# Decoder block with a 16,384-expert mixer on one core: other dense tiles, another pacing of the gathers, sums of the dense experts kept in PSUM

## The chip, the cores and the metric

One core of one Trainium2 chip runs the whole kernel in one launch. The metric is device time in microseconds, the median of several runs. A difference of about 1% is what a measurement of this kernel can tell from no change.

## What is computed

One decoder layer over 1,024 tokens of width 1,024, all in float32. Three token mixers (stick-breaking attention, dilated attention, attention to 256 memory tokens) share one normalised input, are gated by sigmoids, summed and projected. Then comes the expert mixer, which fills most of the time:

```python
q = (hf @ w_q).reshape(T, PEER_HEADS, 2, PEER_HALF)          # 8 heads, two halves of 128
sc = jnp.einsum('thpd,hpkd->thpk', q, subkeys)               # 128 sub-keys for each half
# top 16 of each half, top 16 of their 256 sums -> idx (T, 8, 16) of 16,384 experts, gate = softmax
act = jax.nn.gelu(jnp.einsum('chkd,cd->chk', u[ic], hc), approximate=False)
w = (gc * act)
out = jnp.einsum('chk,chkd->cd', w, v[ic])                   # u, v: (16384, 1024) float32
```

Each token takes 128 of the 16,384 experts: 128 rows of `u` and 128 rows of `v`, 4 KB each.

## The kernel before

The tokens are 8 tiles of 128. The **front** (everything up to the choice of experts) runs in three groups of tiles, `GROUPS = (2, 3, 3)`: tiles 0 and 1, 2 to 4, 5 to 7. Within a group the stages follow one another: norm, `stick_breaking`, `dilated` with `memory_attn`, `gating` (24 gate projections and 24 branch projections), `out_proj`, `ffn_norm`, `select` (query projection and scores). The top-k work of a group's later tiles runs as a side generator (`topk`, in `side`), a piece at each fill, after the group's `select`.

The expert mixer is done in two ways.

- **Six sparse tiles** go through `Experts`. One step takes one expert slot of 128 rows: GpSimd gathers 128 rows of `u` and 128 rows of `v` by indirect DMAs (line 1090, 512 KB each), VectorE multiplies and sums `u` with the token (line 1144), ScalarE applies Gelu, TensorE adds the weighted `v` rows up (line 1170). A tile has 128 steps, all six 768. A step's rows lie in rings of 5 and 6 buffers.
- **Two dense tiles**, `DENSE = (4, 6)`, are multiplied by all 16,384 experts in 128 blocks of 128 experts (`dense`). A block takes 24 matmuls of 256 columns (line 1188, the u product: each float32 operand is split in two parts, a high and a low one, and three partial products are taken), Gelu, a product with the gate matrix, and 12 matmuls of 512 columns (the v sums). The splits are a ScalarE copy and a VectorE subtraction (line 1269). Every two blocks the sums are added from PSUM to the tile `acc` (line 1317).

The gate matrix of a dense tile holds the weight of each expert for each token (`gate_matrix`): for every token two one-hot rows are made on VectorE (lines 1213 and 1215), multiplied on TensorE, copied by ScalarE into a tile `g` and written to DRAM as `gd`, in 4 blocks of 32 tokens; the dense loop loads `gd` back. The matrix of tile 4 is made inside the gating and `out_proj` stages of the third group (`rest`, which lets `want` count the dense tiles of earlier groups); that of tile 6 after the front, in `dense`, before the 128 blocks. Those fills have no other filler work: only gather steps run beside them.

All engines take their instructions in program order, and the order is written by a planner (the last loop of the kernel). It keeps two clocks, `pe` and `dma`: every fill adds its estimated TensorE time times `slow` to the one and its loaded bytes over `bw` to the other; every gather step adds `TOKEN_NS` and `TOKEN_BYTES / bw`.

```python
            while filler[0] is not None and (dma > pe or pe < due):
                a, b = fill(1)
                pe += a
                dma += b
            pe += TOKEN_NS
            dma += TOKEN_BYTES / bw[0]
            if ex.step():
```

So a stage of P ns of estimated TensorE time and M bytes of loads gets about (P x slow - M / bw) / (TOKEN_BYTES / bw - TOKEN_NS) gather steps. Steps that are left when the fillers have ended run alone. PSUM has 5 rotating banks (`bank`), 3 more belong to the gathers.

Of the kernel before, what the change touches and what calls it, by code (L numbers as in the profile page):

```python
# [7 lines left out]
F32 = mybir.dt.float32  # L8
# [3 lines left out]
AF = mybir.ActivationFunctionType  # L12
# [5 lines left out]
D = 1024  # L18
T = 1024
NT = T // 128  # L20
KD = D // 128
# [6 lines left out]
F32R = mybir.dt.float32r  # L28
MANUAL = dict(engines={mybir.EngineType.Activation})
GROUPS = (2, 3, 3)  # L30
DENSE = (4, 6)
ND = len(DENSE)
PAUSE = 4
LAG = 1


BW = 295.0, 360.0
SLOW = 1.38, 1.1
TOKEN_NS, TOKEN_BYTES = 700.0, 128 * 8192 + 3 * 8192.0
LEAST = 3000.0  # L40
SPLIT = (0,)
AHEAD = 2
# [34 lines left out]
def block_kernel(ctx: ExitStack, tc: tile.TileContext, io):  # L77
    nc = tc.nc
# [24 lines left out]
    TD = ND * 128  # L103
    cost = [0.0]
# [3 lines left out]
    def bank():  # L108
        return ps.tile([128, 512], F32, name="bank")
# [12 lines left out]
    def actf(out, in_, f, **kw):  # L122
        s = SETS.get(f)
        if s and table[0] != s:
            nc.scalar.preload_act_table_set(s)  # L125
            table[0] = s
        nc.scalar.activation(out, in_, f, **kw)  # L127
# [50 lines left out]
    gofs, gwid, gnum, o = [], [], [], 0  # L178
# [54 lines left out]
    xres = dram.tile([NT, 128, D], F32, name="xres")  # L233
# [3 lines left out]
    gd = dram.tile([TD // 32, 128, 128, 32], F32, name="gd")  # L237
# [7 lines left out]
    def load(out, src):  # L245
        count(out)
        nc.sync.dma_start(out, src)
# [762 lines left out]
    def phase1(gidx, n0, G, out):  # L1010
        N = G * 128
        pipe = Pipe()
        weights = Weights(gidx)
        hT = wide.tile([128, 8, NMAX], F32, name="wide")
        load(hT[:, :, :N], io["xT"][:, :, n0 * 128:n0 * 128 + N])
        norm = norm_T(hT, N, g_mix, hT)
        if gidx == 0:
            memT = big.tile([128, 8, MEM], F32, name="big")
            load(memT, io["memT"])
            mh = big.tile([128, 8, MEM], F32, name="big")  # L1020
            yield from norm_T(memT, MEM, g_mem, mh)
            kv = memory_kv(pipe, weights, both(gidx, mh, MEM))
            next(kv)
            next(norm)
            yield next(kv)
            next(norm)
            yield next(kv)
            yield next(kv)
            hT = both(gidx, hT, N)
            yield from kv  # L1030
            weights.ahead = AHEAD
            gap_tables()
        else:
            yield from norm
            hT = both(gidx, hT, N)
        oT = act.tile([128, 10, NMAX], F32, name="oT")
        yield from stick_breaking(pipe, weights, hT, n0, G, oT)
        mem = memory_attn(pipe, weights, hT, n0, G, oT)
        yield from dilated(pipe, weights, hT, n0, G, oT, mem)
        yield from mem  # L1040
        mT = wide.tile([128, 8, NMAX], F32, name="wide")
        pipe.flush()
        yield from gating(pipe, weights, hT, N, oT, mT)
        x2 = wide.tile([128, GMAX, D], F32, name="wide")
        yield from out_proj(weights, mT, n0, G, x2)
        h2T = [big.tile([128, 8, NS], F32, name="big") for _ in subs(G)]
        yield from ffn_norm(x2, n0, G, h2T)
        yield from select(pipe, weights, both(gidx, h2T, N), n0, G, out)
# [137 lines left out]
    def mmr(out, lhsT, rhs, **kw):  # L1186
        cost[0] += rhs.shape[-1] / 2.4 + 3
        nc.tensor.matmul(out, lhsT, rhs, **kw)  # L1188
# [51 lines left out]
    C = 2  # L1240

    def dense():
        st = ctx.enter_context(ExitStack())
        dp = st.enter_context(tc.tile_pool(name="dp", bufs=2))
        late_pool.append(dp)
        while len(stored) < ND:
            cost[0] += 1500
            yield
        hh = dp.tile([128, KD, TD], F32R, name="hh", bufs=1)
        hl = dp.tile([128, KD, TD], F32R, name="hl", bufs=1)  # L1250
        acc = dp.tile([128, ND, D], F32, name="acc", bufs=1)
        for i in range(ND):
            r = dp.tile([128, KD, 128], F32, name="ur")
            load(r, h2d[i])
            c = slice(i * 128, (i + 1) * 128)
            actf(hh[:, :, c], r, AF.Copy)
            nc.vector.tensor_sub(hl[:, :, c], r, hh[:, :, c])
            load(acc[:, i, :], xres[DENSE[i]])

        def raw(src, name):  # L1260
            r = dp.tile([128, C, D], F32, name=name)
            load(r, src)
            return r

        def split(r, x, name, bufs):
            hi = dp.tile([128, D], F32R, name=name + "h", bufs=bufs)
            lo = dp.tile([128, D], F32R, name=name + "l", bufs=bufs)
            actf(hi, r[:, x], AF.Copy)
            nc.vector.tensor_sub(lo, r[:, x], hi)  # L1269
            return hi, lo  # L1270

        us, vs, ws = {}, {}, {}
        ur = {0: raw(io["uT"][0], "ur")}
        us[0] = split(ur[0], 0, "u", 2)
        while next(gates) < ND:
            cost[0] += 800
            yield
        for c in range(128 // C):
            if c + 1 < 128 // C:
                ur[c + 1] = raw(io["uT"][c + 1], "ur")  # L1280
            vr = raw(io["vd"][c], "vr")
            for x in range(C):
                e = c * C + x
                if e % 8 == 0:
                    gt = dp.tile([128, TD // 32, 8, 32], F32, name="g")
                    load(gt, gd[:, :, e:e + 8, :].rearrange("b p i t -> p b i t"))
                if e + 1 < 128:
                    us[e + 1] = split(ur[(e + 1) // C], (e + 1) % C, "u", 2)
                vs[x] = split(vr, x, "v", C)
                uh, ul = us.pop(e)  # L1290
                a = bank()
                for k in range(KD):
                    kc = slice(k * 128, (k + 1) * 128)
                    mmr(a[:, :TD], uh[:, kc], hh[:, k, :], start=k == 0, stop=False)
                    mmr(a[:, :TD], ul[:, kc], hh[:, k, :], start=False, stop=False)
                    mmr(a[:, :TD], uh[:, kc], hl[:, k, :], start=False, stop=k == KD - 1)
                w = dp.tile([128, TD], F32, name="w")
                actf(w, a[:, :TD], AF.Gelu)
                nc.vector.tensor_mul(w.rearrange("p (b t) -> p b t", t=32),
                                     w.rearrange("p (b t) -> p b t", t=32), gt[:, :, e % 8, :])  # L1300
                wh = dp.tile([128, TD], F32R, name="wh", bufs=C)
                wl = dp.tile([128, TD], F32R, name="wl", bufs=C)
                actf(wh, w, AF.Copy)
                nc.vector.tensor_sub(wl, w, wh)  # L1304
                ws[x] = wh, wl
                yield
            for i in range(ND):
                for half in range(2):
                    o = bank()
                    f = slice(half * 512, (half + 1) * 512)  # L1310
                    for x in range(C):
                        wh, wl = (z[:, i * 128:(i + 1) * 128] for z in ws[x])
                        vh, vl = (z[:, f] for z in vs[x])
                        mmr(o, wh, vh, start=x == 0, stop=False)
                        mmr(o, wh, vl, start=False, stop=False)
                        mmr(o, wl, vh, start=False, stop=x == C - 1)
                    nc.vector.tensor_add(acc[:, i, f], acc[:, i, f], o)  # L1317
                    yield
        for i in range(ND):
            nc.sync.dma_start(io["out"][DENSE[i]], acc[:, i, :])  # L1320

    ready, side, stored, late_pool = [], [], [], []

    def sides(n):
        while n and side:
# [4 lines left out]
    gates = gate_matrix()  # L1330

    def rest():
        n0 = built = 0
        odd = False
        for g in range(len(GROUPS)):
            for stage in phase1(g, n0, GROUPS[g], ready):
                if stage and built < ND:

                    want = sum(n < n0 for n in DENSE)
                    while len(stored) < want:  # L1340
                        sides(1)
                    odd = not odd
                    for _ in range(999 if stage == 2 else 1 + odd):
                        if built < want:
                            built = next(gates)
                yield
            n0 += GROUPS[g]
        front.close()
        slow[0], bw[0] = SLOW[1], BW[1]
        yield from dense()  # L1350

    filler = [rest()]
    slow, bw = [SLOW[0]], [BW[0]]
    pe = dma = due = 0.0

    def fill(nside):
# [12 lines left out]
    while done < NT - ND or filler[0] is not None:  # L1369
        if ex.more():  # L1370

            due = max(due + LEAST, pe - LEAST)
            while filler[0] is not None and (dma > pe or pe < due):
                a, b = fill(1)
# [66 lines left out]
```

## Time and profile before

| | us |
|---|---|
| three runs | 3843.71, 3854.40 (median), 3871.12 |
| the profiled execution: its own time | 3814.17 |
| its span | 3812.4 |
| front of the first group, no gathers | 0 to 500 |
| fronts of the second and third group, with gathers | 500 to 2525 |
| gate matrix of tile 6 | 2525 to 2745 |
| the 128 dense blocks | 2745 to 3615 |
| gather steps alone | 3615 to 3812 |

The stages were placed by the first and last start of their VectorE lines. The profile gives for any stretch the busy time of each engine, the granted TensorE clock (PEclk, 1.00 is full speed), the mean busy share of the 16 DMA engines and what they moved in GB/s. Matmuls are pipelined, so that a busy TensorE need not be at its peak.

### The profile page before, as it was taken

The numbers are of one execution on the slowest core, as the hardware profiler recorded it, in microseconds if no ns is written. First come the engines' busy times: TensorE is split into PE (matmuls) and PEld (weight loads), VectorE is DVE, ScalarE is ACT, GpSimd is POOL, SyncE is SP. The second block draws the span as 40 slices with busy tenths as digits, with TensorE's granted clock in tenths as the row PEclk, the third lists the DMA queues.
The fourth block names the chain that finished last, engine by engine and source line by source line (L and its number), as shares of the span: only waits on it lengthen the run. The fifth ranks groups of instructions, "written<-read, shape, count | busy, mean of one in ns | idle before, by whom it ended". The sixth has DMA issues, their size and how long they took to land.

```text
span 3812.4 us, 61678 instructions
## 1 busy us (share of the span) xinstructions
PE 3276.5 (86%) x23106; PEld 2403.4 (63%) x23106; DVE 2542.9 (67%) x6405; ACT 1402.9 (37%) x2769; POOL 1712.1 (45%) x1544
## 2 busy tenths in 40 slices
PE   7999778988999798879898998864699999999944
PEld 6889755655556575656555556642478878888700
DVE  5443785555444478875555655699788888888844
ACT  4442435544211225555443222222344444444400
POOL 0000045646566465645454555553633434334476
PEclk9999888999999899989898999885799999999955
DMA  4345578889799997879897999877989999999899
GB/s 153 119 122 168 191 258 305 329 282 356 281 397 395 343 393 268 326 266 322 292 349 268 378 362 376 327 277 274 342 327 366 367 348 362 366 375 369 330 372 345
DMA packets 347010, 1186.38 MB, mean 311 GB/s; under 512 B 38808, under 2 KB 80792, under 8 KB 327256
## 3 DMA queue, kind: packets, MB, share of 16 engines
q0 software_dynamic: 221184, 805.40, 56.9%
q1 hardware_dynamic: 102960, 338.34, 24.8%
q10 hardware_dynamic: 22568, 38.70, 2.7%
q8 instruction: 182, 2.98, 0.3%
q14 instruction: 116, 0.95, 0.1%
HBM read 1142.58 MB, written 39.71 MB: 310 GB/s over the span
## 4 chain that ended last, share of the span: by engine, by line
PE 56%; DVE 16%; issue 10%; DMA 8%; ACT 4%; POOL 3%; another core or an unknown queue 2%; ACTq 1%; POOLq 0%; SPq 0%; DVEq 0%
PE bank L116 29%; PE bank L1188 17%; PE po L1170 6%; DVE u L1144 5%; DMA u<-in_u,iT 2%; DMA v<-in_v,iT 2%; PE pb L1083 2%; POOL v L1090 1%; POOL u L1090 1%; PE bank L120 1%; ACT e L127 1%; DMA ur<-in_uT 1%; DMA gd<-g 1%; DVE ul L1269 1%
## 5 line engine op out<-in xcount | busy, mean ns | idle before, releaser
L1090 POOL DMA_INDIRECT u<-in_u,iT x768 | 867.1, 1129 | 1268.9 <-DVE i L860 504.6
L1090 POOL DMA_INDIRECT v<-in_v,iT x768 | 844.2, 1099 | 820.3 <-PE po L1170 616.8
L1144 DVE SCALAR_TENSOR_TENSOR u<-u,hb 128x1024 f32<-128x1024 f32 x768 | 926.1, 1222 | 411.7 <-ACT hb L127 193.9
L1170 PE MATMUL po<-v,wz 128*32 128x256 f32 x6144 | 464.7, 422 | 135.1 <-DMA v<-in_v,iT 83.8
L116 PE MATMUL bank<-wide,w 128*128 128x384 f32 x1536 | 523.3, 495 | 4.1 <-DVE rs L326 4.1
L116 PEld LDWEIGHTS bank<-wide,w 128*128 128x128 f32 x1536 | 295.0, 194 | 205.8 <-issue 12.1
L1170 PEld LDWEIGHTS po<-v,wz 128*32 128x32 f32 x6144 | 188.9, 116 | 372.2 <-DMA v<-in_v,iT 108.7
L127 ACT ACTIVATE hb<-pb 128x512 f32<-128x512 f32 x384 | 209.6, 593 | 462.8 <-PE pb L1083 185.6
L1188 PE MATMUL bank<-hh,ul 128*128 128x256 f32 x1024 | 290.8, 284 | 2.7 <-DVE ul L1269 2.7
L1188 PE MATMUL bank<-hh,uh 128*128 128x256 f32 x1024 | 292.5, 286 | 0.5 <-ACT uh L127 0.5
L1188 PE MATMUL bank<-hl,uh 128*128 128x256 f32 x1024 | 290.7, 284 | 0.0
L116 PE MATMUL bank<-w,wide 128*128 128x128 f32 x2304 | 272.0, 277 | 12.2 <-issue 9.4
L116 PEld LDWEIGHTS bank<-w,wide 128*128 128x128 f32 x2304 | 266.5, 193 | 21.5 <-issue 14.0
L1188 PE MATMUL bank<-vh,wh 128*128 128x512 f32 x512 | 211.4, 414 | 24.2 <-ACT wh L127 23.4
L127 ACT ACTIVATE e<-bank 128x512 f32<-128x512 f32 (+2 forms) x208 | 109.3, 526 | 316.9 <-PE bank L116 176.8
L1188 PE MATMUL bank<-vl,wh 128*128 128x512 f32 x512 | 202.4, 395 | 0.0
L1188 PEld LDWEIGHTS bank<-hh,ul 128*128 128x128 f32 x1024 | 196.6, 192 | 6.8 <-DVE ul L1269 3.5
L1188 PEld LDWEIGHTS bank<-hh,uh 128*128 128x128 f32 x1024 | 196.6, 192 | 6.9 <-issue 1.6
L1188 PE MATMUL bank<-vh,wl 128*128 128x512 f32 x512 | 197.6, 394 | 1.0 <-DVE wl L1304 0.9
L1188 PEld LDWEIGHTS bank<-hl,uh 128*128 128x128 f32 x1024 | 196.7, 192 | 2.5 <-issue 1.6
L125 ACT ACT_TABLE_LOAD x144 | 184.8, 1283 | 24.1 <-issue 9.2
L1317 DVE TENSOR_TENSOR acc<-acc,bank 128x512 f32<-128x512 f32 x256 | 165.6, 682 | 32.6 <-PE bank L1188 32.5
(290 smaller groups left out, 5969.6 us busy)
## 6 DMA issues: line engine op xcount, KB each, us to landing
ur<-in_uT SPq DMA_DIRECT2D x64, 1024.0 KB
vr<-in_vd SPq DMA_DIRECT2D x64, 1024.0 KB
w<-in_w_in SPq DMA_DIRECT2D x102, 512.0 KB
w<-in_w_gate SPq DMA_DIRECT2D x72, 512.0 KB
w<-in_w_pq SPq DMA_DIRECT2D x48, 512.0 KB
g<-gd SPq DMA_DIRECT2D x16, 1024.0 KB
w<-in_w_o SPq DMA_DIRECT2D x48, 256.0 KB
w<-in_w_out SPq DMA_DIRECT2D x24, 512.0 KB
```

The source lines that it names most:

```text
L116: nc.tensor.matmul(out, lhsT, rhs, **kw)
L120: nc.tensor.transpose(out, in_, ident)
L125: nc.scalar.preload_act_table_set(s)
L127: nc.scalar.activation(out, in_, f, **kw)
L1083: nc.tensor.matmul(pb, which[:, jj].rearrange("p q s -> p (q s)"), box["b3"][:, f], start=True, stop=True)
L1090: nc.gpsimd.indirect_dma_start(out=t, out_offset=None, in_=io[kind], in_offset=bass.IndirectOffsetOnAxis(ap=ap, axis=0))
L1144: nc.vector.scalar_tensor_tensor(u, u, 1.0, self.hb, op0=OP.mult, op1=OP.mult, accum_out=self.parts[:, i:i + 1])
L1170: nc.tensor.matmul(po[32 * k:32 * k + 32, h:h + 256], wz[:, i, :], v[:, 256 * k:256 * k + 256], start=jj == 0 and i == 0, stop=jj == QB - ...
L1188: nc.tensor.matmul(out, lhsT, rhs, **kw)
L1269: nc.vector.tensor_sub(lo, r[:, x], hi)
L1317: nc.vector.tensor_add(acc[:, i, f], acc[:, i, f], o)
```

## The change

Four things are altered.

1. The dense tiles are 5 and 6, both of the third group. `want` is then zero in every group, so no gate matrix is made inside the front, and the gathered tiles are 0, 1, 2, 3, 4, 7.
2. The planner's constants: `bw` differs by group, `slow` by stage, and `TOKEN_NS` is 600.
3. Both gate matrices are made in `dense` ahead of the blocks; at every seventh fill there the u product of a dense block is put (22 in all, `RUN`), and its Gelu result is kept in one of 24 tiles `w`. In the main loop the u product runs 22 blocks ahead of the v sums, and the weights and the split of `v` one block ahead.
4. The v sums stay in four PSUM banks over all 128 blocks (`sums`), the u products of the main loop use the two halves of the fifth (`ab`); `acc` and its additions are gone. At the end `xres` is loaded and added once.

```diff
-DENSE = (4, 6)
+DENSE = (5, 6)
-BW = 295.0, 360.0
-SLOW = 1.38, 1.1
-TOKEN_NS, TOKEN_BYTES = 700.0, 128 * 8192 + 3 * 8192.0
+BW = 330.0, 330.0, 360.0, 345.0
+SLOW = dict(norm=1.3, stick=1.5, dilated=1.27, gating=1.0, proj=1.15, gates=1.0, dense=1.1)
+RUN = 22
+TOKEN_NS, TOKEN_BYTES = 600.0, 128 * 8192 + 3 * 8192.0
...
+        slow[0] = SLOW["stick"]
         yield from stick_breaking(pipe, weights, hT, n0, G, oT)
...
-            load(acc[:, i, :], xres[DENSE[i]])
...
+        def product(e, a):
+            if e + 1 < 128:
+                take(e + 1)
+            uh, ul = us.pop(e)
+            for k in range(KD):
+                ...
+            w = ws[e] = dp.tile([128, TD], F32, name="w", bufs=RUN + 2)
+            actf(w, a, AF.Gelu)
...
-        while next(gates) < ND:
-            cost[0] += 800
-            yield
+        while more or e < RUN:
+            more = more and next(gates) < ND
+            steps += 1
+            cost[0] += 600
+            if e < RUN and (steps % 7 == 0 or not more):
+                product(e, bank()[:, :TD])
+                e += 1
+            yield
+        while side:
+            yield
+        slow[0] = SLOW["dense"]
+        sums = [[bank() for _ in range(2)] for _ in range(ND)]
+        ab = bank().rearrange("p (x n) -> p x n", x=2)
...
+        gate_load(0)
+        vr[0] = raw(io["vd"][0], "vr")
+        now = weigh(0)
+        for e in range(128):
+            if e + RUN < 128:
+                product(e + RUN, ab[:, e % 2, :])
+                yield
+            nxt = weigh(e + 1) if e < 127 else None
+            wh, wl, vh, vl = now
             for i in range(ND):
                 for half in range(2):
-                    o = bank()
+                    o = sums[i][half]
...
-                    nc.vector.tensor_add(acc[:, i, f], acc[:, i, f], o)
-                    yield
+                yield
+            now = nxt
```

`weigh` multiplies a block's Gelu results by the gate matrix, splits the product and splits the block of `v`; `take` splits the next block of `u`; `gate_load` loads eight blocks of `gd` one turn ahead.

More of the change, by code (lines that the diff above doesn't have):

```diff
@@ L1013, in phase1 @@
         weights = Weights(gidx)
+        slow[0], bw[0] = SLOW["norm"], BW[gidx]
         hT = wide.tile([128, 8, NMAX], F32, name="wide")
@@ L1036, in phase1 @@
         oT = act.tile([128, 10, NMAX], F32, name="oT")
+        slow[0] = SLOW["stick"]
         yield from stick_breaking(pipe, weights, hT, n0, G, oT)
+        slow[0] = SLOW["dilated"]
         mem = memory_attn(pipe, weights, hT, n0, G, oT)
@@ L1042, in phase1 @@
         pipe.flush()
+        slow[0] = SLOW["gating"]
         yield from gating(pipe, weights, hT, N, oT, mT)
+        slow[0] = SLOW["proj"]
         x2 = wide.tile([128, GMAX, D], F32, name="wide")
@@ L1245, in dense @@
         late_pool.append(dp)
+        slow[0], bw[0] = SLOW["gates"], BW[3]
         while len(stored) < ND:
@@ L1250, in dense @@
         hl = dp.tile([128, KD, TD], F32R, name="hl", bufs=1)
-        acc = dp.tile([128, ND, D], F32, name="acc", bufs=1)
         for i in range(ND):
-            r = dp.tile([128, KD, 128], F32, name="ur")
+            r = dp.tile([128, KD, 128], F32, name="vr")
             load(r, h2d[i])
@@ L1263, in raw, with split @@
             return r
-        def split(r, x, name, bufs):
-            hi = dp.tile([128, D], F32R, name=name + "h", bufs=bufs)
-            lo = dp.tile([128, D], F32R, name=name + "l", bufs=bufs)
+        def split(r, x, name):
+            hi = dp.tile([128, D], F32R, name=name + "h")
+            lo = dp.tile([128, D], F32R, name=name + "l")
             actf(hi, r[:, x], AF.Copy)
@@ L1270, in split @@
             return hi, lo
-        us, vs, ws = {}, {}, {}
-        ur = {0: raw(io["uT"][0], "ur")}
-        us[0] = split(ur[0], 0, "u", 2)
-        while next(gates) < ND:
-            cost[0] += 800
-            yield
[L1278 to L1305, printed above, removed]
@@ new lines, in dense, with take @@
+        ur, us, ws, vr, gts = {}, {}, {}, {}, {}
+        def take(e):
+            if e % C == 0:
+                ur[e // C + 1] = raw(io["uT"][e // C + 1], "ur") if e + C < 128 else None
+            us[e] = split(ur[e // C], e % C, "u")
+        def product(e, a):
[3 more added lines that the diff above has]
+            for k in range(KD):
+                kc = slice(k * 128, (k + 1) * 128)
+                mmr(a, uh[:, kc], hh[:, k, :], start=k == 0, stop=False, skip_group_check=True)
+                mmr(a, ul[:, kc], hh[:, k, :], start=False, stop=False, skip_group_check=True)
+                mmr(a, uh[:, kc], hl[:, k, :], start=False, stop=k == KD - 1, skip_group_check=True)
+            w = ws[e] = dp.tile([128, TD], F32, name="w", bufs=RUN + 2)
+            actf(w, a, AF.Gelu)
@@ new lines, in dense @@
+        ur[0] = raw(io["uT"][0], "ur")
+        take(0)
+        e = steps = 0
+        more = True
+        while more or e < RUN:
[5 more added lines that the diff above has]
+                e += 1
+            yield
+        while side:
+            yield
+        slow[0] = SLOW["dense"]
+        sums = [[bank() for _ in range(2)] for _ in range(ND)]
@@ new lines, in dense, with gate_load, weigh @@
+        ab = bank().rearrange("p (x n) -> p x n", x=2)
+        def gate_load(b):
+            if b < 16:
+                gts[b] = dp.tile([128, TD // 32, 8, 32], F32, name="g")
+                load(gts[b], gd[:, :, 8 * b:8 * b + 8, :].rearrange("b p i t -> p b i t"))
+        def weigh(e):
+            if e % 8 == 0:
+                gate_load(e // 8 + 1)
+            w = ws.pop(e)
+            nc.vector.tensor_mul(w.rearrange("p (b t) -> p b t", t=32), w.rearrange("p (b t) -> p b t", t=32),
+                                 gts[e // 8][:, :, e % 8, :])
+            wh = dp.tile([128, TD], F32R, name="wh")
+            wl = dp.tile([128, TD], F32R, name="wl")
+            actf(wh, w, AF.Copy)
+            nc.vector.tensor_sub(wl, w, wh)
+            if e % C == 0:
+                vr[e // C + 1] = raw(io["vd"][e // C + 1], "vr") if e + C < 128 else None
+            return wh, wl, *split(vr[e // C], e % C, "v")
@@ L1306, in dense @@
+        gate_load(0)
[4 more added lines that the diff above has]
+                product(e + RUN, ab[:, e % 2, :])
                 yield
+            nxt = weigh(e + 1) if e < 127 else None
+            wh, wl, vh, vl = now
             for i in range(ND):
+                c = slice(i * 128, (i + 1) * 128)
                 for half in range(2):
-                    o = bank()
+                    o = sums[i][half]
@@ L1310, in dense @@
                     f = slice(half * 512, (half + 1) * 512)
[L1311 to L1317, printed above, removed]
@@ L1318, in dense @@
-                    yield
-        for i in range(ND):
-            nc.sync.dma_start(io["out"][DENSE[i]], acc[:, i, :])
+                    mmr(o, wh[:, c], vh[:, f], start=e == 0, stop=False, skip_group_check=True)
+                    mmr(o, wh[:, c], vl[:, f], start=False, stop=False, skip_group_check=True)
+                    mmr(o, wl[:, c], vh[:, f], start=False, stop=e == 127, skip_group_check=True)
+                yield
+            now = nxt
+        for i in range(ND):
+            r = dp.tile([128, C, D], F32, name="ur")[:, 0]
+            load(r, xres[DENSE[i]])
+            for half in range(2):
+                f = slice(half * 512, (half + 1) * 512)
+                nc.vector.tensor_add(r[:, f], r[:, f], sums[i][half])
+            nc.sync.dma_start(io["out"][DENSE[i]], r)
@@ L1322, in block_kernel @@
     ready, side, stored, late_pool = [], [], [], []
+    slow, bw = [1.0], [BW[0]]
     def sides(n):
@@ L1348, in rest @@
         front.close()
-        slow[0], bw[0] = SLOW[1], BW[1]
         yield from dense()
     filler = [rest()]
-    slow, bw = [SLOW[0]], [BW[0]]
     pe = dma = due = 0.0
```

## The prediction

> **What bounds the kernel now.** I read the page's slices first, then the stretches by stage, then the steps in each stretch.
>
> ```profile
> span 3812.4 us, 61678 instructions
> ...
> DVE  5443785555444478875555655699788888888844
> ...
> PEclk9999888999999899989898999885799999999955
> DMA  4345578889799997879897999877989999999899
> ```
>
> Transfers are full in much of the span, but not in three places: the first eighth, where no token has its experts yet, the middle of each group, and slices 27 to 29, where the clock falls too and VectorE is nearly full. Stretches: length, then busy time (and instructions) of TensorE, its weight loads, VectorE, ScalarE and GpSimd, then granted clock, DMA share, GB/s.
>
> ```profile
> 503.00:733.00 230.00, 203.86 (x1391) 140.44 (x1390) 148.46 (x423) 114.07 (x191) 132.23 (x120) 0.92 0.86 314
> 733.00:995.00 262.00, 228.61 (x1758) 146.31 (x1757) 145.77 (x343) 122.03 (x242) 135.53 (x124) 0.92 0.86 311
> 995.00:1211.00 216.00, 214.95 (x1090) 122.32 (x1089) 103.01 (x202) 32.78 (x72) 135.88 (x124) 1.00 0.99 379
> 1211.00:1435.00 224.00, 188.92 (x1504) 153.56 (x1502) 128.88 (x403) 53.41 (x142) 123.83 (x112) 0.93 0.97 374
> 1445.00:1778.00 333.00, 289.22 (x2017) 197.57 (x2016) 254.41 (x800) 180.69 (x288) 182.91 (x162) 0.94 0.81 286
> 1778.00:2047.00 269.00, 238.14 (x1942) 153.73 (x1941) 157.74 (x366) 128.76 (x256) 134.63 (x128) 0.92 0.84 304
> 2047.00:2306.00 259.00, 248.97 (x1356) 151.66 (x1354) 151.09 (x423) 62.34 (x185) 147.27 (x134) 0.98 0.98 365
> 2306.00:2525.00 219.00, 184.15 (x1465) 157.36 (x1465) 147.02 (x568) 48.51 (x138) 116.12 (x103) 0.92 0.93 344
> 2525.00:2745.00 220.00, 115.60 (x780) 69.36 (x779) 195.86 (x729) 61.56 (x180) 107.52 (x92) 0.65 0.78 282
> 2745.00:3615.00 870.00, 839.50 (x5899) 699.15 (x5898) 737.76 (x1153) 382.90 (x628) 346.03 (x304) 0.99 0.94 357
> 3615.00:3812.00 197.00, 91.75 (x606) 18.65 (x605) 88.31 (x167) 19.26 (x49) 139.91 (x130) 0.52 0.96 361
> ```
>
> Rows 1 to 4 and 5 to 8 are stick-breaking, dilated, gating and projection (with selection) of the second and third group; then the matrix of tile 6, the 128 blocks, and the rest of the steps alone. Gating is at both ceilings (TensorE 1.00, DMA 0.99). The attention stages of the third group use 0.81 and 0.84 of the DMA time. The matrix stretch is VectorE's: 195.9 of 220 us. The blocks are TensorE's and nearly DMA's. The last 197 us are DMA's alone. Every us counts, since the stretches follow one another; the question is how many of the 768 steps go where. The steps of a stretch are half the instructions of line 1144 (each has an accumulator read):
>
> ```profile
> 503.00:733.00 230.00, 73.81 (x122) 0.92 0.86 314
> 1445.00:1778.00 333.00, 100.79 (x168) 0.94 0.81 286
> 2047.00:2306.00 259.00, 76.52 (x128) 0.98 0.98 365
> 2525.00:2745.00 220.00, 54.50 (x91) 0.65 0.78 282
> 2745.00:3615.00 870.00, 188.29 (x306) 0.99 0.94 357
> 3615.00:3812.00 197.00, 80.11 (x130) 0.52 0.96 361
> ```
>
> So 61, 84, 64, 45, 153 and 65.
>
> **Pacing.** The front's formula gives the steps of a stage. P and M are counted from the code's cost lines (gating: 272 products of 384 columns at 650 ns, and 96 fills at 50 ns, is 181.6 us of P). The divisor is 2.94 us before in the fronts (3.64 - 0.70), 2.28 after them; in the changed kernel 2.65 in the second group, 2.38 in the third, 2.51 later.
>
> ```
>                   P us           M MB        steps before (formula)  after
> 2nd stick         139.2          8.4         56                      69
> 2nd dilated       166.1          14.4        61                      63
> 2nd gating        181.6          18.1        64                      48
> 2nd proj          152.6 -> 155.8 14.7        55                      51
> 3rd stick         197.1          10.0        81                      113
> 3rd dilated       174.7          15.7        64                      75
> 3rd gating        206.6 -> 181.6 24.4->18.1  69                      55
> 3rd proj          156.2 -> 149.5 16.8->14.7  54                      55
> matrices          120.7 -> 246   11.5->30.4  44                      63
> 128 blocks        688.4 -> 629.4 150->138.4  149                     116
> ```
>
> The formula's 56, 81, 69, 44 and 149 lie near the trace's 61, 84, 64, 45 and 153, so I use it for the change. With two steps in the norms, the changed kernel has 531 steps behind it at the end of the fronts (506 before), 594 after the matrices, 710 after the blocks, and 58 left (65 before). No stage runs dry: two tiles (256 steps) serve the second group, which needs 232, and five (640) last to the end of the matrices.
>
> **What it costs and saves, stretch by stretch.** One step moves 1.07 MB (512 KB twice, and a row of tokens); on TensorE it costs at most 0.56 us: the blocks' 839.5 us less the dense products' own share, by 153.
>
> ```profile
> 2745.00:3615.00 870.00, 754.41 (x4607) 657.41 (x4606) 0.99 0.94 357
> ```
>
> - *Second group.* Stick: 8 steps more than traced bring 72 MB to 81, 214 us at gating's 379 GB/s, so there is room; TensorE's 4.5 us more over its 0.89 share is +5, taken as +8. Dilated: 0. Gating: 16 steps less at 0.56 us of a full TensorE, -9, taken as -10. Projection: -5.
> - *Third group.* Stick: 95 MB (333 us at 286) and 29 to 32 steps more are some 129 MB: 341 us at 379 GB/s, 353 at 365. I take 352, +19, as VectorE and TensorE go up to some 0.85 of it too. Dilated: +4. Gating: the matrix of tile 4 goes, so it falls to the second group's 216 us less 9 steps of 0.56, 211: -48. Projection: 224 is the second group's time; with no matrix left in it I take -12 from 219.
>
> Fronts: 8 + 0 - 10 - 5 + 19 + 4 - 48 - 12 = **-44 us**; bounds -85 (the steps fit into the idle transfers) and -10 (the attention stages stretch by the whole DMA time of their steps).
>
> *Matrices.* VectorE's groups of the stretch that made the one matrix:
>
> ```profile
> L1144 DVE SCALAR_TENSOR_TENSOR u<-u,hb 128x1024 f32<-128x1024 f32 x46 | 55.8, 1213 | 1.0 <-DMA u<-in_u,iT 1.0
> L1213 DVE TENSOR_SCALAR ab<-iota,sl 128x128 f32<-128x128 f32 x128 | 45.3, 354 | 9.8 <-PE bank L116 6.9 <-PE po L1170 1.8 <-PE pb L1083 1.0
> L1215 DVE TENSOR_SCALAR ab<-iota,sl 128x128 f32<-128x128 f32 x128 | 36.9, 288 | 0.0
> ```
>
> The second matrix adds 45.3 + 36.9 = 82 us there (some 64 if the records overlap as the stretch's do: its durations sum to 1.3 times its busy time), 22 splits of u at 1.22 us add 27, 18 steps at 1.3 add 23. So 195.9 becomes 310 to 328 us; at the stretch's 0.89 that is 345 to 368. I take 345, **+125**; bounds +65 (no idle time, overlapped records) and +180. TensorE has room: 115.6 us of 220, to which come one more matrix (about 50), 18 steps, and 22 u products. One u product at full clock is 24 matmuls, 2.87 us:
>
> ```profile
> 3006.14 0.28 PE L1188 MATMUL bank<-hh,uh 128*128 128x256 f32 x1
> ...
> 3009.01 0.28 PE L1188 MATMUL bank<-hh,uh 128*128 128x256 f32 x1
> ...
> 3011.64 0.39 PE L1188 MATMUL bank<-vh,wh 128*128 128x512 f32 x1
> ...
> 3013.49 0.39 PE L1188 MATMUL bank<-vh,wl 128*128 128x512 f32 x1
> ```
>
> That is 63 us, or 97 at the granted 0.65: TensorE sums to under 280 of 345 us, so the products hide behind VectorE. If that cover were gone they would cost up to 97. The Trainium skill (TensorE: Matmul & The Clock Gate, "What's actually happening") says that the clock is either full or half, and that a short busy window opens it; by half clock the 22 products would be an estimated 126 us and still hidden. The trace's 0.65 for 53% busy is a mean that such a gate could give.
>
> *Blocks.* 8 matmuls of the sums take 1.85 us (3011.64 to 3013.49), so 12 take 2.78 and a block 5.65 at best; the row above gives 754.4 / 128 = 5.89. With 0.99 steps, 6.2 to 6.45 us; the block's 1.18 MB and its steps are 2.25 MB, 6.3 us at 357 GB/s. I take 6.3 for 106 blocks, 668. The last 22 have no u product: 2.78 + 0.24 on TensorE, 1.11 MB, 3.1 us each, 68. Ahead of the first sums stands the reload of the last matrix, which stays:
>
> ```profile
> 2712.41 13.15 DMA gd<-g
> ...
> 2745.78 7.95 DMA gd<-g
> 2753.78 14.69 DMA g<-gd
> ```
>
> That is 25 us with the new `gate_load(0)`. Behind it on SyncE's queue wait the first load of `v` and the token rows of the steps; the u loads are past. Sum 761 against 870, **-109** (bounds -145 at 6.0 us a block, -70). The 256 additions I cost at nothing: VectorE is at 738 of 870 and
>
> ```profile
> L1317 DVE TENSOR_TENSOR acc<-acc,bank 128x512 f32<-128x512 f32 x256 | 165.6, 682 | 32.6 <-PE bank L1188 32.5
> ```
>
> waited for TensorE, not TensorE for it. Late next are the DMA share and TensorE. At most their going saves the blocks' excess over 5.65 us a block, inside the bounds above.
>
> *Rest.* 58 steps for 65 at 197 / 65 = 3.03 us: **-21**. The load of `xres` and four additions lie beside them.
>
> Sum: -44 + 125 - 109 - 21 = -49, a span of 3763 from 3812. The profiled execution took 3814.17, 40 less than the median of the runs, so the same share goes off 3854.4: **3805**, a gain of 1.3%, hardly more than the 1% that a measurement can tell from no change.
>
> **Rivals.**
>
> - *The fronts give nothing* (0.27). The transfers were idle in attention for a reason other than pacing; the 30 extra steps stretch the stage by 30 x 2.83 us, 85 rather than 19. Against it: gating held 0.99. It gives -49 + 66, about 3870, within 1%.
> - *More than forecast* (0.20). The matrices take 290 us, the blocks 6.0: -49 - 55 - 32, about 3715. For it: the overlap of VectorE's records and blocks prepared one ahead.
> - *Slower: the blocks of the gate matrices* (0.12). The changed kernel makes all 8 blocks of 32 tokens from one pool with two `g` tiles, and a block takes both, so it waits until both `gd` writes have landed (8 to 13 us above, behind which ScalarE's copies for the gather steps stand in its queue). Half of them used the front's larger pool before. Now 12 MB of u loads share the time. My 345 us has some 33 us for a block. From 33 + 49 / 8 = 39 us the gain is gone; at 50, as much again as a write's longest wait, it is +87, about 3940.
> - *Product waits for Gelu* (0.04). In the list of waits, total us, times and the longest:
>
> ```profile
> ACT w L127 <- PE bank L1188: 168.7, 60, 7.4
> ```
>
>   All later u products write the halves of one bank, while ScalarE reads the other half. The row speaks against a cost: ScalarE waits for TensorE, and 2.78 us of sums lie between two products. If ScalarE's queue made it 4 us, 106 x 1.2 us would go, about 3930. The Trainium skill (PSUM — Partial Sum Buffer, "PSUM bank collisions raise a hardware error") says that two engines must be kept apart by bank, not by address, which is what would make this wait; no run here shows it yet.
>
> **How the numbers follow.** The forecast has 0.37, with 3770 to 3835 as its own range. Below 3816 lie some 0.25 of it and the gain rival, with a corner of the first rival: faster 0.50. Same takes the rest of the forecast and most of the first rival: 0.33. Slower: 0.17. The range runs from 3705 to 3895: it takes in the gain and the no-gain rival and leaves out the worse half of the slower ones.
>
> **What would show it.** Steps by stretch as in the table; third-group gating near 211 us with no line 1213 in it; a matrix stretch near 345 us with VectorE near 0.9 and a clock over 0.65; blocks at 6.3 us with DMA over 0.93; under 60 steps alone. Wrong would be: a front longer than 1980 us after 490, ScalarE waiting on `gd` for over 100 us, or TensorE waiting on Gelu in the blocks.

## The result, and the profile after

The changed kernel took 3897.1 us (median of 4 runs, 3885 to 3907) beside 3850.1 for the one before: a ratio of 1.0111, interval 1.0062 to 1.016. It is slower by 1.1%, where 3805 had been forecast. The profiled execution has a span of 3883.4 us, 71 more than before. Its page, the same rows as before:

```profile
span 3883.4 us, 61596 instructions
...
DVE  5443785565434557975556444689886666776653
...
DMA  4345479989799896899989899985888999999898
```

VectorE's last quarter falls from 8 to 6 and 7, since the 256 additions are gone. The hole in the transfers at its slice 28 is the begin of the matrices.

The stretches, in the order used for the kernel before (length, busy time and count of TensorE, weight loads, VectorE, ScalarE, GpSimd, then clock, DMA share, GB/s): four of the second group, four of the third, the matrices, the 128 blocks, the steps alone.

```profile
503.00:755.00 252.00, 220.63 (x1463) 135.59 (x1461) 159.93 (x446) 118.29 (x200) 154.43 (x141) 0.93 0.91 331
755.00:1023.00 268.00, 235.63 (x1797) 149.02 (x1796) 153.95 (x361) 123.70 (x248) 145.40 (x131) 0.92 0.87 319
1023.00:1228.00 205.00, 204.97 (x987) 118.44 (x986) 82.35 (x161) 27.97 (x60) 102.97 (x96) 1.00 0.93 335
1228.00:1468.00 240.00, 186.21 (x1427) 153.77 (x1426) 132.63 (x409) 54.22 (x141) 115.84 (x104) 0.89 0.89 332
1478.00:1873.00 395.00, 332.90 (x2270) 204.37 (x2269) 280.48 (x854) 201.72 (x320) 237.70 (x216) 0.89 0.87 311
1873.00:2172.00 299.00, 259.35 (x2112) 151.90 (x2114) 176.18 (x400) 133.83 (x267) 167.25 (x159) 0.93 0.91 332
2172.00:2385.00 213.00, 212.50 (x1053) 120.69 (x1045) 90.91 (x181) 31.97 (x69) 120.89 (x110) 0.99 0.94 352
2385.00:2610.00 225.00, 190.14 (x1508) 156.00 (x1508) 153.79 (x622) 47.98 (x132) 129.97 (x117) 0.91 0.94 356
2610.00:2952.00 342.00, 230.53 (x1644) 181.07 (x1644) 286.40 (x967) 126.11 (x356) 138.43 (x125) 0.81 0.80 291
2952.00:3707.00 755.00, 732.47 (x5012) 624.87 (x5012) 511.05 (x782) 338.39 (x556) 295.20 (x226) 0.98 0.93 343
3707.00:3883.00 176.00, 77.82 (x536) 16.54 (x536) 78.47 (x150) 15.82 (x41) 118.06 (x111) 0.53 0.92 343
```

The steps are again half the instructions of the product line (now 1150):

```profile
1023.00:1228.00 205.00, 57.32 (x96) 1.00 0.93 335
1478.00:1873.00 395.00, 129.65 (x214) 0.89 0.87 311
3707.00:3883.00 176.00, 71.17 (x116) 0.53 0.92 343
```

From the matrices on, everything came out within 6 us of the forecast: 342 us for the matrices, 755 for the blocks, 58 steps alone in 176 us. The loss lies in the fronts, which end at 2610 us and not at 2525. Third stick-breaking, with 107 steps for 84, went from 333 to 395 us, the dilated stage from 269 to 299; second stick-breaking grew by 22. And while it has 0.87 of the DMA time, third stick-breaking moves 311 GB/s, not the 379 of gating.

### The profile page after: what moved, and what is told of

Its sections match the earlier page's. It is cut to its first block, busy times and chain, and to the rows that moved or that the text cites. A ratio compares the mean times of both kernels' runs of the same rounds, so it can differ in the third digit from the quotient of the medians.

```text
span 3883.4 us, 61596 instructions
## 1 busy us (share of the span) xinstructions
PE 3318.6 (85%) x23106; PEld 2407.5 (62%) x23106; DVE 2391.2 (62%) x6153; ACT 1415.3 (36%) x2787; POOL 1732.1 (45%) x1544
## 3 DMA queue, kind: packets, MB, share of 16 engines
q8 instruction: 182, 2.98, 0.3%
## 4 chain that ended last, share of the span: by engine, by line
PE 40%; DVE 8%; issue 6%; DMA 6%; ACT 3%; POOL 1%; another core or an unknown queue 1%; ACTq 0%; SPq 0%; POOLq 0%; DVEq 0%
PE bank L1194 17%; PE bank L117 17%; PE po L1176 5%; DVE u L1150 2%; DMA gd<-g 1%; PE pb L1089 1%; DMA v<-in_v,iT 1%; ACT e L128 1%; POOL v L1096 1%; DVE ab L1219 1%; POOL u L1096 1%; DMA w<-in_w_pq 1%; DMA b3d<-wide 0%; DVE ab L1221 0%
## 5 line engine op out<-in xcount | busy, mean ns | idle before, releaser
L1096 POOL DMA_INDIRECT u<-in_u,iT x768 | 878.6, 1144 | 1267.2 <-DVE i L861 499.6
L1176 PE MATMUL po<-v,wz 128*32 128x256 f32 x6144 | 478.2, 420 | 150.9 <-DMA v<-in_v,iT 75.2
L117 PE MATMUL bank<-wide,w 128*128 128x384 f32 x1536 | 536.0, 497 | 9.6 <-DVE wide L340 9.0
L1176 PEld LDWEIGHTS po<-v,wz 128*32 128x32 f32 x6144 | 172.0, 115 | 398.4 <-issue 124.6
L1194 PEld LDWEIGHTS bank<-hh,uh 128*128 128x128 f32 x1024 | 205.0, 200 | 21.1 <-issue 12.4
L1194 PEld LDWEIGHTS bank<-hh,ul 128*128 128x128 f32 x1024 | 204.5, 200 | 5.6 <-DVE ul L1274 1.4
L117 PE MATMUL bank<-big,w 128*128 128x128 f32 (+1 forms) x1024 | 181.6, 336 | 14.4 <-DMA w<-in_w_pq 10.9
```

The lines of the kernel that those rows point to most:

```text
L1096: nc.gpsimd.indirect_dma_start(out=t, out_offset=None, in_=io[kind], in_offset=bass.IndirectOffsetOnAxis(ap=ap, axis=0))
L1176: nc.tensor.matmul(po[32 * k:32 * k + 32, h:h + 256], wz[:, i, :], v[:, 256 * k:256 * k + 256], start=jj == 0 and i == 0, stop=jj == QB - ...
```

## The experiments

Theory: the new pacing took steps out of stretches where a step is cheap and put them into attention, where it is dear. Rivals: the rest of the change stretches attention; or a step's cost is ScalarE's switching of tables. The runs were made on several chips. By the record the kernel before took 3651 us on chip 11 both times that it was used, 3811 on chip 8 and 3653 on chip 5; for the 3850 us of the result no chip is on record. So ratios are formed only between runs measured together, and times of stages are compared on one chip.

**The pacing undone, and the pacing alone.**

```diff
-BW = 330.0, 330.0, 360.0, 345.0
-SLOW = dict(norm=1.3, stick=1.5, dilated=1.27, gating=1.0, proj=1.15, gates=1.0, dense=1.1)
+BW = 295.0, 295.0, 295.0, 360.0
+SLOW = dict(norm=1.38, stick=1.38, dilated=1.38, gating=1.38, proj=1.38, gates=1.1, dense=1.1)
...
-TOKEN_NS, TOKEN_BYTES = 600.0, 128 * 8192 + 3 * 8192.0
+TOKEN_NS, TOKEN_BYTES = 700.0, 128 * 8192 + 3 * 8192.0
```

> The changed kernel with the constants of before (bw 295 in all groups and 360 after, slow 1.38 and 1.1, a step at 700 ns); tiles, order of the matrices, early u products and PSUM sums stay. The plan then gives 55, 62, 64, 56 steps to the stages of the second group, 81, 64, 65, 53 to those of the third, 81 to the matrices, about 133 to the blocks. Theory (the pacing moved steps from gating, where one costs some 0.6 us, into attention, where one costs 2 to 3): the third group's stick-breaking falls from 395 to near 333 us, its dilated stage from 299 to near 270, both gating stages lie at 211 to 216, matrices 365, blocks 770, 52 steps alone 157; span near 3765, about 1% under the kernel before. Rival (the other dense tiles and the order of their work stretch the attention stages, not the pacing): third stick-breaking stays over 375 us with 81 steps, span over 3850.

The ratio to the kernel before was 1.0002 (0.9987 to 1.0016). The opposite, the kernel before with the new constants set at the same places:

> The kernel before with nothing but the new constants by group and stage. The plan gives 110 and 77 steps to the third group's attention stages, 48 and 59 to the gating stages, and the rows run dry at 512 steps in the third projection. Theory (pacing): stick-breaking of the third group near 395 us, dilated near 299, gating of the second group near 205; some 95 steps stay for the end, 290 us; slower than before by 2 to 4%. Rival (structure): third stick-breaking under 350 us, time within 1% of before.

1.0316 (1.0296 to 1.0336): pacing by itself costs more than the whole change lost on this chip (1.0224, below). Its third stick-breaking took 360 us, and 95 steps in 268 us were left for the end. Part of that is peculiar to this run: its pacing uses up the chosen rows in the third projection, where 37 steps stand in 251 us at a DMA share of 0.69. And the rest of the change, forecast at some -45 us, gave nothing; see the three kernels on one chip below.

**What makes a step dear.** First ScalarE's tables:

```diff
-                    actf(ge, parts, AF.Gelu)
+                    actf(ge, parts, AF.Copy)
```

> The changed kernel with a copy in place of the Gelu of the gather steps, so that ScalarE needn't switch tables for them in attention (two loads of 1.28 us for four steps); the output is not the reference's. If the table switches make a step dear in attention, the third stick-breaking falls by 40 to 69 us (27 groups of four steps, 2.57 us each) and the dilated stage by 30 or more. If the transfers do, both change by less than 15 us.

```profile
L126 ACT ACT_TABLE_LOAD x10 | 12.8, 1283 | 0.2
```

The table loads fell from 162 (208 us) to 10, and third stick-breaking stayed at 367 us with 109 steps (370 with as many for the changed kernel on chip 11, below). That rival falls. Then half the bytes:

```diff
-            nc.gpsimd.indirect_dma_start(out=t, out_offset=None, in_=io[kind],
+            nc.gpsimd.indirect_dma_start(out=t[:, 512:] if kind == "u" else t[:, :512], out_offset=None,
+                                         in_=io[kind].rearrange("e (x n) -> (e x) n", n=512),
...
-                                         v[:, 256 * k:256 * k + 256], start=jj == 0 and i == 0,
+                                         v[:, 256 * (k % 2):256 * (k % 2) + 256], start=jj == 0 and i == 0,
```

> The changed kernel with gathers of half rows (256 KB instead of 512 KB each, the product and the sums use the half twice, so that the engines' instructions keep their counts and sizes); its output is not the reference's. If the price of a step in attention is its transfer, the third stick-breaking falls from 395 to 330 us or less with the same 107 steps, and the steps alone take 1.5 us each instead of 3.03. If the price is ScalarE's table switches or the order on the engines, it stays over 375 us and only the steps alone get faster.

Third stick-breaking and the steps alone, all engines:

```profile
1380.00:1716.00 336.00, 306.64 (x2345) 205.82 (x2344) 285.93 (x872) 207.77 (x328) 259.61 (x225) 0.95 0.68 211
3431.00:3604.00 173.00, 76.20 (x537) 15.68 (x536) 78.97 (x152) 15.85 (x41) 129.66 (x112) 0.53 0.61 179
```

Stick-breaking took 336 us with 113 steps, 31 less than the run above on the same chip; but the steps alone did not get faster at all: 58 in 173 us, with transfers at 0.61. GpSimd there makes one gather after another, with 0.3 us between two:

```profile
3502.56 1.52 POOL L1096 DMA_INDIRECT v<-in_v,iT  x1 [0.30 <-issue]
3504.39 0.95 POOL L1096 DMA_INDIRECT u<-in_u,iT  x1 [0.30 <-issue]
3505.65 1.41 POOL L1096 DMA_INDIRECT v<-in_v,iT  x1 [0.30 <-issue]
```

3.09 us from one v to the next (2.98 on the average of the 58 steps) is a step's whole price alone. The smaller rows are not neutral for GpSimd: alone, a gather of `v` keeps it busy for 1.34 us on average, against 0.99 with whole rows. In stick-breaking, 259.6 us busy and 0.3 us before each of 225 gathers are 327 of 336 us. So with half rows GpSimd may have taken over as the bound, which a run with fewer steps tests (stick-breaking at 1.17, chip 11 again):

> Gathers of half rows together with stick-breaking at 1.17 (some 88 steps in the third stick-breaking instead of 113); the output is not the reference's. With half rows GpSimd was at its issue 98% of that stage. If its issue sets the price of a step, 24 steps less make the stage shorter by 24 x 2.97 = 70 us (to some 265). If the order on the other engines does, it falls by 35 us or less (to 300).

```profile
1350.00:1649.00 299.00, 108.32 (x182) 0.98 0.64 194
```

91 steps in 299 us, 37 less for 22 steps fewer: short of the 70 that GpSimd's issue alone would give, just over the 35 of the other engines. With whole rows the stage takes 298 us with 87 steps on this chip (below), so near 90 steps bytes hardly matter: TensorE is busy 283 of those 298 us, and 285 of the 299 with half rows. Above that number, whole rows cost about 3.3 us a step and half rows 1.7. Halving the bytes takes away half of the price, so at least half of it goes with the bytes. How the 1.7 us that stay divide into transfers, GpSimd and TensorE (busy 22 us more with the 22 steps) these runs don't show.

**Changed, before and old constants on one chip (chip 11).**

> The kernel before, for its stretches on the chip of this call.

> The changed kernel on the chip of this call. Pacing theory: over before by as much as the steps' hosts make it, 1.2 to 2.4%; third stick-breaking 2.6 to 2.8 us longer for each of the 25 steps more.

> The changed kernel with the old constants on the same chip. By the prediction's own terms for what is not pacing it gains some 45 us over before: third gating -48, third projection -12, matrices +125, the 128 blocks -109 less some 18 for the additional steps, the end -35. If it comes out equal to before, one of these terms falls short by 40 us or more: the candidates are the matrices (over 370 us from the end of the projection) and the blocks (over 790).

The changed kernel: 1.0224 (1.0197 to 1.0251) on this faster chip; with the old constants 0.999 (0.9974 to 1.0006). Steps (half the count), clock, DMA share and GB/s of the kernel before in second gating, third stick-breaking, third dilated, blocks, alone:

```profile
967.00:1181.00 214.00, 76.71 (x126) 1.00 1.01 393
1406.00:1700.00 294.00, 101.12 (x168) 0.98 0.91 332
1700.00:1949.00 249.00, 77.39 (x128) 0.96 0.90 327
2630.00:3465.00 835.00, 183.92 (x297) 0.99 0.94 359
3465.00:3655.00 190.00, 82.73 (x136) 0.54 0.98 383
```

The changed kernel (the matrices, from the dense tiles' split on, are the fourth row):

```profile
981.00:1185.00 204.00, 54.30 (x92) 1.00 0.94 342
1424.00:1794.00 370.00, 132.30 (x218) 0.92 0.93 341
1794.00:2073.00 279.00, 98.13 (x162) 0.94 0.94 347
2530.00:2837.00 307.00, 69.33 (x114) 0.83 0.84 308
2837.00:3575.00 738.00, 138.36 (x228) 0.99 0.93 345
3575.00:3734.00 159.00, 71.40 (x116) 0.53 0.98 380
```

With the old constants:

```profile
961.00:1175.00 214.00, 77.05 (x128) 1.00 1.01 393
1415.00:1713.00 298.00, 104.70 (x174) 0.99 0.92 333
1713.00:1960.00 247.00, 72.97 (x120) 0.95 0.88 325
2424.00:2760.00 336.00, 91.12 (x150) 0.84 0.90 337
2760.00:3506.00 746.00, 159.43 (x262) 0.99 0.96 367
3506.00:3643.00 137.00, 60.39 (x98) 0.52 0.97 382
```

Between the last two only the place of the steps differs, so they price a step by its place: 72 us for 22 steps in third stick-breaking (3.3 us), 32 for 21 in dilated (1.5), 10 for 18 in gating (0.6), 29 for 18 beside the matrices (1.6), 8 for 17 in the blocks (0.5), 2.8 alone. With the old constants third stick-breaking takes 298 us with 87 steps, beside 294 with 84 in the kernel before: the rest of the change doesn't stretch it.

All engines in third stick-breaking, with the old constants and in the changed kernel:

```profile
1415.00:1713.00 298.00, 282.69 (x2109) 194.78 (x2107) 254.60 (x807) 185.24 (x296) 195.32 (x169) 0.99 0.92 333
1424.00:1794.00 370.00, 326.48 (x2345) 201.58 (x2344) 284.13 (x864) 205.87 (x328) 246.50 (x220) 0.92 0.93 341
```

With the old constants TensorE is busy 0.95 of the stage, as in the kernel before on this chip (281 of 294 us). So the idle share of the transfers stood beside a nearly full TensorE. The 22 added steps raise TensorE's busy time by 44 us, 2 us each where the prediction took 0.56, and the granted clock falls from 0.99 to 0.92.

Once more, on the chip of the best version below:

> The changed kernel with the old constants once more, for its stretches beside those of before. If the pacing is all of the loss: third stick-breaking 330 us with 81 steps, 52 steps alone; time between 0.5% under before and the same. If the other dense tiles or the order of the matrices cost something that the pacing hides: 1% over before.

The ratio was 0.9992 (0.9978 to 1.0005), so the same three times. Between the first and the last of the three tables the pacing is alike: third gating came down from 245 to 213 us (-32, forecast -48), the blocks by 89 and the end by 53, and second projection grew by 15 with nearly the same steps (56 and 57). From the end of third gating to the begin of the blocks, before and with the old constants:

```profile
2194.00:2630.00 436.00, 116.36 (x192) 0.79 0.87 326
2173.00:2760.00 587.00, 164.57 (x272) 0.85 0.91 341
```

This stretch, with third projection and the matrices in it, grew by 151 us. The prediction's -12 and +125, with its 1.3 us for each of 12 steps more than its 63, make +129. So the shortfall stands in no single place: third gating gave 16 less, this stretch cost 22 more and second projection 15, while the end gave 18 more than the 35 expected. In the stretch's last 336 us VectorE (0.81 busy) carries two matrices, the splits of u and the 40 added steps.

**Steps put back where they are cheap.** On chip 8, with the attention pacing left as it was:

```diff
-SLOW = dict(norm=1.3, stick=1.5, dilated=1.27, gating=1.0, proj=1.15, gates=1.0, dense=1.1)
+SLOW = dict(norm=1.3, stick=1.5, dilated=1.27, gating=1.17, proj=1.15, gates=1.2, dense=1.165)
```

> The changed kernel with three constants altered: gating 1.0 to 1.17, gates 1.0 to 1.2, dense 1.1 to 1.165; the attention pacing stays. The plan then gives 59 and 69 steps to the gating stages (48 and 55), 82 to the matrices (63), 131 to the blocks (117) and none is left for the end (58). Theory (a step costs 0.6 us in gating, about 1.5 beside the matrices, 0.3 in the blocks and 2.8 alone): gating +15 us together, matrices +28, blocks +10, the end -160: some 110 us less than the changed kernel, and faster than before by 0.5 to 1%. Rival (a step costs the same wherever it is put, because transfers set the time): the end goes, but the other stretches grow by as much; within 30 us of the changed kernel.

0.9898 (0.9871 to 0.9924) of the kernel before. The changed kernel beside it:

> The changed kernel once more, so that its stretches can be set against those of the other runs of this call. Theory (pacing): 2 to 2.5% slower than before on a chip that takes about 3650 us for before; steps by stretch as in the plan: 69, 63, 48, 50, then 109, 78, 55, 55, then 63, 117 and 58 alone; third stick-breaking near 365 us. Rival (the first measurement of +1.1% holds everywhere): 1.0 to 1.2%.

1.0145 (1.011 to 1.018) here, 3866 us; so 99 us less with three constants. The kernel before on this chip:

> The kernel before once more, for its stretches on this chip. Theory: third stick-breaking near 300 us with 81 steps, blocks near 840 us with 150 steps, 65 steps alone at 2.8 us, 183 us.

It had 84 steps in 329 us of third stick-breaking, the changed kernel 109 in 398: 2.8 us a step. The changed kernel's two gating stages, matrices, blocks and end:

```profile
1031.00:1236.00 205.00, 53.87 (x92) 1.00 0.94 341
2169.00:2376.00 207.00, 64.52 (x108) 1.00 0.99 369
2637.00:2948.00 311.00, 69.36 (x114) 0.83 0.83 304
2948.00:3692.00 744.00, 137.86 (x228) 0.99 0.92 343
3692.00:3870.00 178.00, 71.23 (x116) 0.53 0.92 340
```

and with the three constants:

```profile
1027.00:1235.00 208.00, 68.03 (x116) 1.00 1.00 380
2164.00:2394.00 230.00, 81.14 (x134) 0.98 1.00 385
2660.00:3009.00 349.00, 90.21 (x148) 0.79 0.87 322
3009.00:3758.00 749.00, 155.12 (x256) 0.99 0.94 357
```

12 steps cost 3 us in second gating; 13 cost 23 in third gating, where the DMA share is at 1.00; 17 cost 38 beside the matrices, 14 cost 5 in the blocks. The 58 steps alone, 178 us, are gone.

**Is the long attention the loss?** Only stick-breaking changed, 1.5 to 1.17:

> The changed kernel with stick-breaking at 1.17 in place of 1.5: 51 and 86 steps there instead of 69 and 109, and some 45 more alone at the end. If a step costs about as much in stick-breaking (2.8 us) as alone (3.0), the two stages lose 115 us and the end gains 135: the whole stays within 25 us of the changed kernel. If the long attention stages are themselves the loss against before, it gains 70 to 100 us and comes below before.

1.0283 (1.0258 to 1.0307), on chip 5. Third stick-breaking and the end:

```profile
1396.00:1701.00 305.00, 108.41 (x180) 0.98 0.93 340
3471.00:3758.00 287.00, 125.56 (x204) 0.52 0.98 379
```

The stage is short again, 305 us, and 102 steps stand at the end in 287 us. The changed kernel was not measured on this chip; on chip 11, where the kernel before takes as long, it had 1.0224. A step in stick-breaking costs about what it costs alone (2.8 us), so taking it out of attention to the end gains nothing.

**The sums in PSUM alone,** in the kernel before:

```diff
...
+        sums = [[bank() for _ in range(2)] for _ in range(ND)]
+        ab = bank().rearrange("p (x n) -> p x n", x=2)
...
-                a = bank()
+                a = ab[:, x, :]
...
-                    o = bank()
+                    o = sums[i][half]
...
-                    nc.vector.tensor_add(acc[:, i, f], acc[:, i, f], o)
...
```

> The kernel before with its dense sums kept in four PSUM banks and the u products in the halves of the fifth; the 256 additions to acc are gone, the top-k of the last tile is ended ahead of the blocks, all else stays. If the additions cost nothing, as the prediction has it: blocks within 15 us of those of before, time within 0.5%. If VectorE's 166 us of additions hold the blocks back: blocks 40 us shorter or more, time 1% less. If products wait for Gelu in the shared bank: blocks longer by 50 us or more.

1.0056 (1.003 to 1.0082), so it costs. The blocks of the kernel before on that chip, and those of this one, with the wait of TensorE's weight loads for Gelu in them:

```profile
2760.00:3605.00 845.00, 830.89 (x5794) 692.25 (x5798) 729.97 (x1139) 379.62 (x622) 336.39 (x293) 0.99 0.93 355
```

```profile
2766.00:3632.00 866.00, 851.27 (x5786) 689.95 (x5786) 590.73 (x890) 387.97 (x622) 376.94 (x294) 0.99 0.92 347
...
PEld bank L1188 <- ACT w L127: 39.2, 62, 2.7
```

VectorE has 139 us less to do and the blocks are 21 us longer. Two products stand back to back here, and the second waits for the Gelu that reads the other half of its bank, in 62 places; in the kernel before this wait does not occur. The weight loads, which run ahead of their products, wait 39 us for it, and the products themselves 10; so the wait accounts for part of the 21 us, and the rest is open. Whether the additions' going alone would have saved something can't be read from a run in which the wait came with it.

**The best version found:**

```diff
-SLOW = dict(norm=1.3, stick=1.5, dilated=1.27, gating=1.0, proj=1.15, gates=1.0, dense=1.1)
+SLOW = dict(norm=1.3, stick=1.4, dilated=1.33, gating=1.17, proj=1.15, gates=1.2, dense=1.2)
```

> As the run with cheap hosts, with stick-breaking 1.5 to 1.4, dilated 1.27 to 1.33 and dense 1.165 to 1.2: the plan moves 6 and 6 steps out of the two stick-breaking stages (63 and 104), puts 4 and 2 more into the dilated stages and some 6 more into the blocks; none is left alone. Theory: 12 x 2.8 us less in stick-breaking, some 5 us more in dilated, 3 to 8 in the blocks: 20 us under the run with cheap hosts, about 1.5% under before. Rival (the blocks are at the transfers' ceiling with 128 steps): no better than the run with cheap hosts, 1.0% under before.

0.9859 (0.9841 to 0.9877) of the kernel before, 3597.3 us beside 3652.7. It beats the kernel before, and with it the changed kernel, which was slower than the kernel before wherever they were measured together. That it also beats the run with cheap hosts (0.9898) isn't shown: they ran on different chips.

## Why the prediction was wrong

- *Steps by stretch: right within 6 steps.* Forecast 69, 63, 48, 51, 113, 75, 55, 55, 63, 116 and 58; the trace has 70, 66, 48, 52, 107, 80, 55, 57, 61, 114 and 58.
- *Third stick-breaking, "95 MB and 29 to 32 steps more are some 129 MB: 341 us at 379 GB/s": the step that failed.* Forecast +19 us, measured +62. The rate of gating was taken for a stage that reaches 311 GB/s with 107 steps on this chip and 341 on a faster one. The added steps cost 2.7 us each, close to the 2.83 of the no-gain rival, which gave 85 us for 30 steps. TensorE's part of a step was mis-sized too: at 0.56 us, taken from the blocks, 23 steps are 13 us, and TensorE was busy 44 us longer (289 and 333), with the clock at 0.89 for 0.94. The 43 us between forecast and measurement are the largest part of a miss of 120 (forecast -49, span +71).
- *Third dilated +4, measured +30; second stick-breaking +8, measured +22; second dilated 0, measured +6.* The same step failed: an idle share of the transfers was read as room. For third dilated the runs on chip 11 show it (32 us for 21 steps); for the other two it is inferred. The four attention stages make 89 of the 120 us.
- *Second projection -5, measured +16 up to the next group; third projection -12, measured +6.* Second projection grew by 15 with the old constants too, so there it is not the pacing. The cause stays open in both.
- *Third gating -48: -46. Second gating -10: -11. Matrices 345 us: 342. Blocks 761: 755. End -21: -21.* Right, and as far as busy times tell the u products hid behind VectorE (286 of 342 us busy, TensorE 231, clock 0.81). Fronts in all: forecast -44, measured +85; the sign "a front longer than 1980 us after 490" came, with 2120.
- *The rival of the gate matrices' blocks:* it didn't come. ScalarE waited 34 us in all for the writes to `gd`, 6.1 at the longest.
- *The 256 additions at nothing:* not contradicted, since without them the blocks of the PSUM run were no shorter; but the wait for Gelu came in with that run, so it is not shown either. *The products' wait for Gelu in the shared bank:* in the changed kernel's blocks TensorE's longest wait is another, the first one for `v`, and none is for Gelu, since 2.8 us of sums lie between two products. Where they don't, the wait is there. The Trainium skill (PSUM — Partial Sum Buffer, "PSUM bank collisions raise a hardware error") has two engines kept apart by bank, not by address; the 62 waits agree with that, as the Gelu reads the other half of the bank. A collision itself no run here shows.

```profile
PEld bank L1194 <- ACT vh L128: 27.0, 6, 19.6
```

- *"The last 197 us are DMA's alone": half right.* On chip 11 the DMA share there is 0.97 to 0.98, but GpSimd's issue is close behind: 0.99 and 1.05 us for the two gathers and 0.3 before each are 2.6 of a step's 2.8 us. With half rows the end didn't shorten.
- *Slips in the working, without effect on the outcome:* 310 us at 0.89 are 348 and not 345; blocks at 6.0 us give -141 and not -145; the 33 us for a block of the gate matrices aren't worked out (345 / 8 are 43).

What the prediction didn't do was to compare places. Each of the 768 steps goes somewhere; lowering gating from 1.38 to 1.0 moved 16 and 10 steps out of stages in which one costs some 0.6 us (measured in the second), and raising stick-breaking put them where one costs 2.7 to 3.3. The sum carried their number on rightly, and priced their new place by another stage's rate.

Open: why third stick-breaking with its added steps fills neither the transfers (0.87 to 0.93) nor TensorE (0.84 to 0.88), and why one chip's stage is 13% slower than another's. Neither was tried.

## What to carry to other kernels

When work can be put beside several stages, price one piece in each stage from two runs that differ only in its place, and fill the cheapest first: here 0.5 us in the blocks, 0.6 in gating up to a full DMA share, 1.5 in dilated attention, 1.6 to 2.2 beside the matrices, 2.7 to 3.3 in stick-breaking. An idle share of one resource is not room by itself: here it stood beside a TensorE that was busy 0.87 to 0.95 of the stage, and the rate of another stage was not reached. A stage's limit is seen when more pieces are put into it: on chips 5 and 11 third stick-breaking took 84 to 90 steps in 294 to 305 us, and on chip 11 it needed 3.3 us for each one above 87.

## What the hardware showed beyond what was expected

- Gathers of half rows took at least as long per step as whole ones when nothing else ran (2.98 us and 2.8): GpSimd needs 0.93 to 1.5 us to make a gather of 128 rows and 0.3 us between two.
- The same kernel differed by 5% from one chip to another (3651 to 3850 us), and half of that lay in the attention stages (77 of 157 us between two profiles): third stick-breaking took 294 us on one, 333 on another, both with 84 steps. With it the cost of the change varied from 1.1 to 2.2%.
